# Attention output projection of an encoder layer: its first half in a fixed order by row blocks, with the last heads' values and turns between them

## The chip, the core and the metric

The kernel runs on one core of one Trainium2 chip. A core has four compute engines with instruction queues of their own: TensorE (matmuls and transposes; PE in the profile, its weight loads PEld), VectorE (DVE), ScalarE (ACT) and GpSimd (POOL). SyncE (SP) issues most of the transfers. Operands lie in the on-chip memory SBUF, matmul results in the eight banks of PSUM. The metric is the time of one execution on the device in microseconds (us); the median of several runs counts, lower is better.

## What is computed

One layer of a bidirectional encoder on 512 tokens of width 1024: two parallel mixers (a state-space branch and a gated MLP branch) merged by gates, then attention to 256 memory tokens, then a SwiGLU feed-forward part (FFN). The change lies in the attention:

```python
def memory_cross_attention(hn, memn, w_q, w_k, w_v, w_o):
    q = (hn @ w_q).reshape(bsz, seq, XATTN_HEADS, XATTN_HEAD_DIM)   # 512 x (4 heads x 256)
    k = (memn @ w_k).reshape(bsz, MEM_LEN, XATTN_HEADS, XATTN_HEAD_DIM)
    v = (memn @ w_v).reshape(bsz, MEM_LEN, XATTN_HEADS, XATTN_HEAD_DIM)
    s = jnp.einsum('blhd,bmhd->bhlm', q, k).astype(jnp.float32) * (XATTN_HEAD_DIM ** -0.5)
    p = jax.nn.softmax(s, axis=-1).astype(v.dtype)
    o = jnp.einsum('bhlm,bmhd->blhd', p, v).reshape(bsz, seq, D_MODEL)
    return o @ w_o
...
        h = h + memory_cross_attention(rms_norm(h, xattn_norm_g[i]), memn,
                                       w_q[i], w_k[i], w_v[i], w_xo[i])
        h = h + swiglu(rms_norm(h, ffn_norm_g[i]), w_gate[i], w_up[i], w_down[i])
    return rms_norm(h, final_norm_g)
```

## The kernel before

Every product is taken in three matmuls (`mm3`, L355): each operand is split into a high part, rounded to the type fp32r, and a low part, the rest; high times high, high times low and low times high are added up. `split` (L83) makes the parts: ACT casts the high one (L85), DVE subtracts it (L86). So each matrix that a product has made passes through ACT and DVE before the next product can read it.

The attention works by heads, four of them. `scores(hd)` (L1402) multiplies queries and keys, and ACT and DVE make the softmax in `prob`, token rows on the partitions. `turn_probs` (L1426) transposes `prob` on TensorE, four 128x128 transposes for each half of the memory tokens, eight for a head, into a bank `ppt`, and splits the result into `p_hi`, `p_lo`. `values` (L1436) multiplies the memory's values `vts` by them, for each of the two blocks of 128 columns of a head (`dt_`): six matmuls into a bank `po`, split into `ot_hi`, `ot_lo`. A head thus makes two of the eight blocks of k of the last product, `ot` times `w_xo`.

That product is done in two halves of 512 output columns. A half has four row blocks of 128 tokens (t), each summed in a bank of its own (`pt0` to `pt3`), and four weight blocks (wi) of two blocks of k each, one for a head. A row block with one weight block is six matmuls of 128x512 (`tok_block`, L431). The first half is done by `tokm` (L1512, L399), which takes the first two weight blocks for all rows, then the last two together for row after row. Between the weight blocks its `hooks` call `second` (values of head 1, turns of heads 2 and 3) and `last_two` (values of heads 2 and 3). At the end of a row `add_evac` (L1328) adds the bank to the residual `h` on DVE, and ACT sums its squares. The second half is written out below it (L1522 on), and goes two rows at a time; behind it come the norm, the transposes of its result (`ptr`) and the FFN.

Weights are taken from a list made beforehand. `next_w` (L330) hands out the next block and on the way issues loads, three blocks ahead, into a ring of three raw buffers (`wraw`), and splits, two blocks ahead, into a ring of three pairs `whi`, `wlo` (L107). A buffer comes free when the last instruction that reads it is done. Blocks 2 and 3 of the second half and the first FFN blocks lie in other buffers (`s`), in a pool that is opened where the heads' pool is closed (L1513 to L1515). SP's queue carries the loads and is in order, like each engine's; POOL's queue carries transfers that add onto a loaded tile, and one small operation of the norm (`r`).

PSUM has two rings: five banks `mm` (`bank`, L77), used by `psc`, `po`, `pt` and the products, and three banks `aux` (L80), used by the transposes.

The order on each engine's queue is not that of the code. A planner orders the instructions of each engine by a simulated clock: of those whose inputs it takes as ready, the one written first. `in_order` (`tc.keep_in_program_order`) pins an instruction behind the one that was written before it for the same engine. In the first half of w_xo nothing is pinned before the change. `tick` moves work of other stages forward; none is left here but a counter.

Of the kernel before, what the change touches and what calls it, by code (L numbers as in the profile page):

```python
# [17 lines left out]
P = 128  # L18
D = 1024
T = 512  # L20
NT = T // P
KD = D // P
M = 256
NM = M // P
# [28 lines left out]
def hybrid_layer_kernel(  # L53
# [8 lines left out]
    nc = tc.nc  # L62
    x, mem, out = x[0], mem[0], out[0]
    w_in, w_glu, w_proj_a, w_proj_b, w_out = w_in[0], s5_w_glu[0], w_proj_a[0], w_proj_b[0], w_out[0]
    w_q, w_k, w_v, w_xo = w_q[0], w_k[0], w_v[0], w_xo[0]
# [11 lines left out]
    def bank(name):  # L77
        return pm.tile([P, 512], F32, tag="mm", name=name)

    def aux(name, shape=(P, 512)):  # L80
        return pa.tile(list(shape), F32, tag="aux", name=name)
# [11 lines left out]
    in_order = tc.keep_in_program_order  # L93
# [261 lines left out]
    def mm3(ps, a, b, start, stop, free=False, turn=False):  # L355

        for i, (x, y) in enumerate(((0, 0), (0, 1), (1, 0))):
            m = nc.tensor.matmul(ps, a[x], b[y], start=start and i == 0, stop=stop and i == 2, skip_group_check=free)  # L358
            if turn:
                in_order(m)  # L360
# [38 lines left out]
    def tokm(w, c0, act, nk, evac, ntok=NT, last=2, kpt=2, hooks={}, cut=None, t0=0):  # L399


        toks = range(t0, t0 + ntok)
        ps = {t: bank(f"pt{t - t0}") for t in toks}
        nw = nk // kpt
        held = []
        full = slice(0, 512)
        for wi in range(nw):
            hi, lo = next_w(w, wi * kpt, kpt, c0, 512)
            held.append((wi, hi, lo))
            if wi in hooks:  # L410
                hooks[wi]()
            if wi < nw - last:
                todo, held = held, []
                for t in toks:
                    end = cut is not None and t == ntok - 1 and wi == nw - last - 1
                    tok_block(ps[t], t, todo, act, kpt, full, wi == 0, end)
                    if end:
                        cut(None, ps[t])
                tick(1.3 * ntok)
        for t in toks:  # L420
            if cut is not None and t == ntok - 1:
                for i in range(2):
                    p = aux("pcut", (P, 256))
                    tok_block(p, t, held, act, kpt, slice(256 * i, 256 * i + 256), True, True)
                    cut(i, p)
            else:
                tok_block(ps[t], t, held, act, kpt, full, nw == last, True)
                evac(t, ps[t])
            tick(1.3 * len(held))

    def tok_block(ps, t, ws, act, kpt, cs, first, final):  # L431
        tsl = slice(t * P, (t + 1) * P)
        for i, (wi, hi, lo) in enumerate(ws):
            for k in range(kpt):
                kk = wi * kpt + k
                mm3(ps, (act[0](kk, tsl), act[1](kk, tsl)) if callable(act[0]) else
                    (act[0][:, kk, tsl], act[1][:, kk, tsl]),
                    (hi[:, k, cs], lo[:, k, cs]), first and i == k == 0,
                    final and i == len(ws) - 1 and k == kpt - 1)

    side = {"gen": None, "credit": 0.0, "rate": 0.0, "now": 0, "later": []}

# [653 lines left out]
    for h in range(H):  # L1096
        ps = bank("psv")
# [230 lines left out]
    def add_evac(half, layer, fin, fin0=None):  # L1328

        def f(t, ps):  # L1330
            nc.vector.tensor_tensor(h[:, t, HALF[half]], h[:, t, HALF[half]], ps, ALU.add)
            sum_sq(hss[:, layer, t, half:half + 1], h[:, t, HALF[half]])
            if half == 1:
                fin(t, hss[:, layer, t, :])
            elif fin0 is not None:
                fin0(t)
        return f
# [85 lines left out]
                nc.vector.tensor_scalar(prob[:, 2 * i + tt, :], prob[:, 2 * i + tt, :], rs[:, tt:tt + 1], None, ALU.mult)  # L1423
        return prob

    def turn_probs(hd, prob):  # L1426
        p_hi = ap_.tile([P, NM, T], F32R, tag="p_hi", name="p_hi", bufs=2)
        p_lo = ap_.tile([P, NM, T], F32R, tag="p_lo", name="p_lo", bufs=2)
        for mt in range(NM):
            ps = aux("ppt", (P, NT, P))  # L1430
            for t in range(NT):
                nc.tensor.transpose(ps[:, t, :], prob[:, t, mt * P:(mt + 1) * P], ident)
            split(p_hi[:, mt, :], p_lo[:, mt, :], ps.rearrange("p t m -> p (t m)"))
        return p_hi, p_lo

    def values(hd, p_hi, p_lo):  # L1436
        for dt_ in range(2):
            ps = bank("po")
            cs = slice(hd * XD + dt_ * P, hd * XD + dt_ * P + P)
            for mt in range(NM):  # L1440
                mm3(ps, (vts[0][:, mt, cs], vts[1][:, mt, cs]), (p_hi[:, mt, :], p_lo[:, mt, :]), mt == 0, mt == NM - 1)
            split(ot_hi[:, 2 * hd + dt_, :], ot_lo[:, 2 * hd + dt_, :], ps)

    def query_product(ps, n, q, start=False):
# [5 lines left out]
    def turn(hd, probs):  # L1450
        pts[hd] = turn_probs(hd, probs)
# [43 lines left out]
    probs3 = scores(3)  # L1495
    turn(1, probs1)

    def second():
        values(1, *pts.pop(1))
        turn(2, probs2)  # L1500
        turn(3, probs3)

    def last_two():
        for i in (2, 3):
            values(i, *pts.pop(i))

    g_f = gain(ffn_norm_g[0], "g_f")
    ot = (ot_hi, ot_lo)
    fn_hi, fn_lo = token_slot("fn", AWAY)
    fn = (fn_hi, fn_lo)  # L1510

    tokm(w_xo, 0, ot, KD, add_evac(0, 1, None), hooks={1: second, 2: last_two})  # L1512
    at.close()  # L1513
    ff = ExitStack()
    fp = ff.enter_context(tc.tile_pool(name="ffn", bufs=1))  # L1515
# [330 lines left out]
```

## Time and profile before

| | us |
|---|---|
| median of 3 runs | 881.05 |
| fastest and slowest run | 880.0, 881.38 |
| the profiled execution | 883.48 |
| its span, first to last instruction | 881.7 |
| mean granted TensorE clock | 0.992 of full speed |

The span is that of the profiled execution alone, and its time is 1.8 us longer. All times of rows are microseconds from the span's start. A row of the timeline gives start, length, engine, line, operation, output and inputs, and in brackets the idle time of the engine just before it with what ended that. The length of a matmul's row is modelled and longer than its pace: rows of neighbouring matmuls overlap. A row of stretches gives start and end, length, and for each engine busy time and number of instructions, then the granted clock, the share of the DMA engines and GB/s.

### The profile page before, as it was taken

The numbers are of one execution on the slowest core, as the hardware profiler recorded it, in microseconds if no ns is written. First come the engines' busy times: TensorE is split into PE (matmuls) and PEld (weight loads), VectorE is DVE, ScalarE is ACT, GpSimd is POOL, SyncE is SP. The second block draws the span as 40 slices with busy tenths as digits, with TensorE's granted clock in tenths as the row PEclk, the third lists the DMA queues.
The fourth block names the chain that finished last, engine by engine and source line by source line (L and its number), as shares of the span: only waits on it lengthen the run. The fifth ranks groups of instructions, "written<-read, shape, count | busy, mean of one in ns | idle before, by whom it ended". The sixth has DMA issues, their size and how long they took to land.

```text
span 881.7 us, 14747 instructions
## 1 busy us (share of the span) xinstructions
PE 863.3 (98%) x5760; PEld 769.7 (87%) x5760; DVE 658.4 (75%) x1068; ACT 467.2 (53%) x692; POOL 86.4 (10%) x117
## 2 busy tenths in 40 slices
PE   8999999999998999999999999999999999999996
PEld 5788888888888988889899878999999999988875
DVE  5699885899845777658856836767878767899875
ACT  5643953244366553547555535645455455656664
POOL 1001301311000001100001001101211111000010
PEclk8999999999999999999999999999999999999999
DMA  7769565898664798735679645647999998366672
GB/s 239 197 191 298 104 179 148 183 234 193 166 195 115 241 285 258 245 112 156 207 218 256 172 108 159 168 123 168 228 232 236 211 239 215 96 187 207 193 237 96
DMA packets 117256, 169.56 MB, mean 192 GB/s; under 512 B 9265, under 2 KB 82497, under 8 KB 117058
## 3 DMA queue, kind: packets, MB, share of 16 engines
q1 hardware_dynamic: 97602, 141.64, 50.6%
q0 software_dynamic: 19296, 26.45, 19.2%
q8 instruction: 45, 0.74, 0.3%
q10 hardware_dynamic: 288, 0.52, 0.2%
q14 instruction: 25, 0.20, 0.1%
HBM read 159.71 MB, written 48.73 MB: 236 GB/s over the span
## 4 chain that ended last, share of the span: by engine, by line
PE 91%; DMA 4%; ACT 2%; DVE 2%; SPq 1%; issue 1%; POOL 0%; POOLq 0%; ACTq 0%; DVEq 0%
PE pf L358 26%; PE pt L358 17%; PE px L1146 12%; PE pq L1146 6%; PE dx L358 5%; PE dq L358 3%; PE pv L1146 3%; PE bx L1146 2%; PE qx L1146 2%; PE dv L358 2%; PE pz L889 2%; PE ptr L520 1%; PE po L358 1%; PE qv L1146 1%; DMA slab<-in_s_log_step_dram 1%; DMA wraw<-qsum 1%
## 5 line engine op out<-in xcount | busy, mean ns | idle before, releaser
L85 ACT CAST whi<-wraw 128x1024 fp32r<-128x1024 f32 (+1 forms) x145 | 148.6, 1025 | 158.0 <-PE pf L358 48.6
L86 DVE TENSOR_TENSOR wlo<-wraw,whi 128x1024 fp32r<-128x1024 f32 (+1 forms) x145 | 171.9, 1188 | 69.1 <-ACT whi L85 67.4
L358 PE MATMUL pf<-xn,whi 128*128 128x512 f32 x448 | 140.4, 393 | 0.0
L358 PEld LDWEIGHTS pf<-xn,whi 128*128 128x128 f32 x448 | 83.7, 188 | 17.5 <-issue 0.4
L358 PE MATMUL pf<-xn,wlo 128*128 128x512 f32 x224 | 87.8, 392 | 0.0
L1146 PE MATMUL px<-fn,whi 128*128 128x256 f32 x480 | 83.3, 276 | 0.0
L1146 PEld LDWEIGHTS px<-fn,whi 128*128 128x128 f32 x480 | 72.6, 188 | 0.2
L86 DVE TENSOR_TENSOR wlo<-b,whi 128x1024 fp32r<-128x1024 f32 x40 | 48.9, 1222 | 27.9 <-ACT whi L85 27.9
L85 ACT CAST whi<-b 128x1024 fp32r<-128x1024 f32 x40 | 42.2, 1054 | 50.8 <-PE px L1146 27.8
L1146 PE MATMUL px<-fn,wlo 128*128 128x256 f32 x240 | 66.4, 277 | 0.0
L1146 PE MATMUL pq<-s,whi 128*128 128x256 f32 x320 | 55.0, 276 | 0.0
L358 PE MATMUL dx<-whi,s 128*128 128x512 f32 x170 | 53.4, 391 | 0.4 <-DVE h L1771 0.4
L86 DVE TENSOR_TENSOR wlo<-t,whi 128x1024 fp32r<-128x1024 f32 x30 | 36.7, 1224 | 19.4 <-ACT whi L85 19.4
L85 ACT CAST whi<-t 128x1024 fp32r<-128x1024 f32 x30 | 31.6, 1053 | 35.3 <-PE pv L1146 12.4
L358 PEld LDWEIGHTS pf<-xn,wlo 128*128 128x128 f32 x224 | 42.1, 188 | 8.7 <-issue 0.2
L1146 PEld LDWEIGHTS pq<-s,whi 128*128 128x128 f32 x320 | 48.2, 188 | 0.0
L358 PE MATMUL pt<-whi,xn 128*128 128x512 f32 x128 | 44.6, 415 | 1.6 <-ACT xn L85 1.4
L1146 PEld LDWEIGHTS px<-fn,wlo 128*128 128x128 f32 x240 | 45.1, 188 | 0.0
L1146 PE MATMUL pq<-s,wlo 128*128 128x256 f32 x160 | 44.2, 276 | 0.0
L358 PEld LDWEIGHTS dx<-whi,s 128*128 128x128 f32 x170 | 31.8, 188 | 7.5 <-issue 0.8
L358 PE MATMUL dx<-wlo,s 128*128 128x512 f32 x85 | 33.1, 391 | 0.3 <-DVE wlo L86 0.3
L358 PEld LDWEIGHTS pt<-whi,xn 128*128 128x128 f32 x128 | 24.7, 195 | 7.8 <-ACT xn L85 2.0
(451 smaller groups left out, 2200.7 us busy)
## 6 DMA issues: line engine op xcount, KB each, us to landing
wraw<-in_w_in_dram SPq DMA_DIRECT2D x36, 512.0 KB, 4.6
dsum<-in_w_down_dram SPq DMA_DIRECT2D x20, 512.0 KB, 5.7
wraw<-dsum SPq DMA_DIRECT2D x20, 512.0 KB, 3.8
b<-in_w_gate_dram SPq DMA_DIRECT2D x15, 512.0 KB, 6.6
b<-in_w_up_dram SPq DMA_DIRECT2D x15, 512.0 KB, 5.6
wraw<-in_w_down_dram SPq DMA_DIRECT2D x15, 512.0 KB, 4.5
dsum<-in_w_down_dram POOLq DMA_DIRECT2D x10, 512.0 KB, 7.8
dsum<-dsum POOLq DMA_DIRECT2D x10, 512.0 KB, 7.6
```

The lines of the kernel that those rows point to most:

```text
L85: hi = nc.scalar.copy(dst_hi, src)
L86: lo = nc.vector.tensor_tensor(dst_lo, src, dst_hi.bitcast(F32), ALU.subtract)
L358: m = nc.tensor.matmul(ps, a[x], b[y], start=start and i == 0, stop=stop and i == 2, skip_group_check=free)
L520: nc.tensor.transpose(ps[:, j, :], src[:, k * P:(k + 1) * P], ident)
L889: nc.tensor.matmul(ps[:, g, :], wt[:, g, :], u[:, o * GO + g, :], start=True, stop=True)
L1146: nc.tensor.matmul(ps[:, j, :], a[x], b[y], start=start and j == k == i == 0, stop=k == 3 and i == 2, skip_group_check=True)
```

## The change

The first half of w_xo is no longer done by `tokm`. Its instructions on TensorE are written out and pinned, through a new argument `turn` of `tok_block`, `turn_probs` and `values`, which is handed on to `mm3` or to `in_order`. The order on TensorE becomes, with S(wi, t) a row block, V(hd, dt) a block of a head's values and T(hd) the eight transposes of a head:

```
S(0,0) V(1,0) S(0,1) V(1,1) S(0,2) T(2) S(0,3)
S(1,0) T(3) S(1,1) V(2,0) S(1,2) V(2,1) V(3,0) S(1,3) V(3,1)
S(2,0) S(3,0)  S(2,1) S(3,1)  S(2,2) S(3,2)  S(2,3) S(3,3)
```

The values written so take their bank from the ring `aux` of three and not from the ring of five. ACT, DVE, POOL and SP are not pinned, nor are the values of head 0, the turns of heads 0 and 1, the scores and the second half.

```diff
--- before.py
+++ after.py
@@ -428,7 +428,7 @@
                 evac(t, ps[t])
             tick(1.3 * len(held))
 
-    def tok_block(ps, t, ws, act, kpt, cs, first, final):
+    def tok_block(ps, t, ws, act, kpt, cs, first, final, turn=False):
         tsl = slice(t * P, (t + 1) * P)
         for i, (wi, hi, lo) in enumerate(ws):
             for k in range(kpt):
@@ -436,7 +436,7 @@
                 mm3(ps, (act[0](kk, tsl), act[1](kk, tsl)) if callable(act[0]) else
                     (act[0][:, kk, tsl], act[1][:, kk, tsl]),
                     (hi[:, k, cs], lo[:, k, cs]), first and i == k == 0,
-                    final and i == len(ws) - 1 and k == kpt - 1)
+                    final and i == len(ws) - 1 and k == kpt - 1, turn=turn)
 
     side = {"gen": None, "credit": 0.0, "rate": 0.0, "now": 0, "later": []}
 
@@ -1423,22 +1423,25 @@
                 nc.vector.tensor_scalar(prob[:, 2 * i + tt, :], prob[:, 2 * i + tt, :], rs[:, tt:tt + 1], None, ALU.mult)
         return prob
 
-    def turn_probs(hd, prob):
+    def turn_probs(hd, prob, turn=False):
         p_hi = ap_.tile([P, NM, T], F32R, tag="p_hi", name="p_hi", bufs=2)
         p_lo = ap_.tile([P, NM, T], F32R, tag="p_lo", name="p_lo", bufs=2)
         for mt in range(NM):
             ps = aux("ppt", (P, NT, P))
             for t in range(NT):
-                nc.tensor.transpose(ps[:, t, :], prob[:, t, mt * P:(mt + 1) * P], ident)
+                m = nc.tensor.transpose(ps[:, t, :], prob[:, t, mt * P:(mt + 1) * P], ident)
+                if turn:
+                    in_order(m)
             split(p_hi[:, mt, :], p_lo[:, mt, :], ps.rearrange("p t m -> p (t m)"))
         return p_hi, p_lo
 
-    def values(hd, p_hi, p_lo):
-        for dt_ in range(2):
-            ps = bank("po")
+    def values(hd, p_hi, p_lo, parts=(0, 1), turn=False):
+        for dt_ in parts:
+            ps = aux("po") if turn else bank("po")
             cs = slice(hd * XD + dt_ * P, hd * XD + dt_ * P + P)
             for mt in range(NM):
-                mm3(ps, (vts[0][:, mt, cs], vts[1][:, mt, cs]), (p_hi[:, mt, :], p_lo[:, mt, :]), mt == 0, mt == NM - 1)
+                mm3(ps, (vts[0][:, mt, cs], vts[1][:, mt, cs]), (p_hi[:, mt, :], p_lo[:, mt, :]), mt == 0, mt == NM - 1,
+                    turn=turn)
             split(ot_hi[:, 2 * hd + dt_, :], ot_lo[:, 2 * hd + dt_, :], ps)
 
     def query_product(ps, n, q, start=False):
@@ -1495,21 +1498,40 @@
     probs3 = scores(3)
     turn(1, probs1)
 
-    def second():
-        values(1, *pts.pop(1))
-        turn(2, probs2)
-        turn(3, probs3)
-
-    def last_two():
-        for i in (2, 3):
-            values(i, *pts.pop(i))
-
     g_f = gain(ffn_norm_g[0], "g_f")
     ot = (ot_hi, ot_lo)
     fn_hi, fn_lo = token_slot("fn", AWAY)
     fn = (fn_hi, fn_lo)
 
-    tokm(w_xo, 0, ot, KD, add_evac(0, 1, None), hooks={1: second, 2: last_two})
+    fin = add_evac(0, 1, None)
+    ps = {t: bank(f"pt{t}") for t in range(NT)}
+    held = []
+
+    def out_rows(wi, t):
+        tok_block(ps[t], t, held[wi:wi + 1], ot, 2, slice(0, 512), wi == 0, wi == 3, True)
+
+    def head_values(hd, dt_):
+        values(hd, *pts[hd], parts=(dt_,), turn=True)
+
+    def head_turn(hd, prob):
+        pts[hd] = turn_probs(hd, prob, True)
+
+    between = {(0, 0): lambda: head_values(1, 0), (0, 1): lambda: head_values(1, 1),
+               (0, 2): lambda: head_turn(2, probs2), (1, 0): lambda: head_turn(3, probs3),
+               (1, 1): lambda: head_values(2, 0),
+               (1, 2): lambda: (head_values(2, 1), head_values(3, 0)), (1, 3): lambda: head_values(3, 1)}
+    for wi in range(2):
+        held.append((wi,) + next_w(w_xo, 2 * wi, 2, 0, 512))
+        for t in range(NT):
+            out_rows(wi, t)
+            tick(1.3)
+            between.get((wi, t), lambda: None)()
+    held += [(wi,) + next_w(w_xo, 2 * wi, 2, 0, 512) for wi in (2, 3)]
+    for t in range(NT):
+        out_rows(2, t)
+        out_rows(3, t)
+        fin(t, ps[t])
+        tick(2.6)
     at.close()
     ff = ExitStack()
     fp = ff.enter_context(tc.tile_pool(name="ffn", bufs=1))
```

## The prediction

> **What bounds the kernel now.** I read the page's first part and its chain of waits first, then a table of stretches around the changed stage, and last the instructions of that stage in order of time. The page says that TensorE works nearly all the span and that the chain runs along it.
>
> ```profile
> PE 863.3 (98%) x5760; PEld 769.7 (87%) x5760; DVE 658.4 (75%) x1068; ACT 467.2 (53%) x692; POOL 86.4 (10%) x117
> PE 91%; DMA 4%; ACT 2%; DVE 2%; SPq 1%; issue 1%; POOL 0%; POOLq 0%; ACTq 0%; DVEq 0%
> ```
>
> The table of stretches (start:end, length, then busy time and count by engine) places the stage: the first half of w_xo runs from 495.5 to 529.7, the second half to 553.4, then the FFN.
>
> ```profile
> core 0: us, PE busy (x) PEld busy (x) DVE busy (x) ACT busy (x) POOL busy (x), PEclk, DMA share, GB/s
> 495.50:529.70 34.20, 33.26 (x154) 26.33 (x153) 16.39 (x30) 14.17 (x28) 2.35 (x2) 1.00 0.48 121
> 529.70:553.40 23.70, 23.70 (x114) 19.65 (x113) 15.72 (x27) 12.86 (x26) 2.98 (x4) 1.00 0.58 159
> 553.40:600.00 46.60, 46.60 (x408) 46.55 (x407) 34.78 (x38) 25.31 (x35) 4.34 (x4) 1.00 0.54 147
> 600.00:700.00 100.00, 100.00 (x885) 100.00 (x884) 77.25 (x78) 52.07 (x63) 14.00 (x13) 1.00 0.91 217
> ```
>
> Behind 529.7 TensorE is never idle here, so a stage that ends x us sooner or later moves the end by x, and nothing that only reaches the other engines sooner is worth anything. Within the stage TensorE is idle for 0.94 us by these rows; that and the pace of its matmuls is all that this change can win.
>
> In order of time (start, length, engine, line, operation; an idle time in brackets) the stage holds these places:
>
> ```profile
> 495.53 0.39 PE L358 MATMUL pt<-whi,ot_hi 128*128 128x512 f32 x1
> 496.90 0.60 PE L1432 MATMUL ppt<-ident,prob 128*128 128x128 f32 x4
> 501.87 0.48 PE L358 MATMUL po<-p_hi,vt 128*128 128x512 f32 x1
> 503.78 0.60 PE L1432 MATMUL ppt<-ident,prob 128*128 128x128 f32 x4
> 504.65 0.50 PE L358 MATMUL pt<-whi,ot_hi 128*128 128x512 f32 x1 [0.27 <-ACT ot_hi L85]
> 513.27 0.39 PE L358 MATMUL po<-p_hi,vt 128*128 128x512 f32 x1
> 514.34 0.50 PE L358 MATMUL pt<-whi,ot_hi 128*128 128x512 f32 x1 [0.68 <-ACT ot_hi L85]
> 525.80 0.39 PE L358 MATMUL po<-p_hi,vt 128*128 128x512 f32 x1
> 528.83 1.07 PE L358 MATMUL pt<-whi,ot_lo 128*128 128x512 f32 x4
> 529.74 0.39 PE L358 MATMUL pt<-whi,ot_hi 128*128 128x512 f32 x1
> 529.74:543.34 13.60, 13.60 (x61) 11.21 (x60) 8.37 (x15) 5.66 (x14) 1.89 (x2) 1.00 0.86 237
> 514.34:529.74 15.40, 15.40 (x67) 12.27 (x68) 6.14 (x8) 5.20 (x7) 1.14 (x1) 1.00 0.63 167
> ```
>
> The first row is the stage's first matmul, the last instruction row the first of the second half: 34.21 us. The last two rows are stretches with no transposes; a count holds one instruction that belongs to the neighbour, so they give 13.60/60 = 0.2267 us for a matmul that runs row block by row block, and 15.40/66 = 0.2333 where the stage goes block of k by block of k, changing bank every other matmul. Both waits are for ot_hi: a head's values had been computed in the one bank left of five, and w_xo ran into them.
>
> **The change, part by part.** No arithmetic is added or removed: 96 matmuls into pt, 36 into po and 20 transposes of head 1 (second half), 2 and 3, before and after. What changes is who stands behind whom on TensorE.
>
> *The two waits.* The bracketed 0.27 and 0.68 are less than the loss, since a matmul's row is longer than its pace. Four transposes take 4 x 0.11 = 0.44 us (the price below), so L358 could have gone on at 504.22 and went at 504.65: 0.43. After the row at 513.27 it could have gone at 513.50 and went at 514.34: 0.84. In the new order the values of a head stand at least one other block ahead of their use, so I take out 0.43 + 0.84 = 1.27. To check the cover, a split of one such result:
>
> ```profile
> 508.62 0.59 ACT L85 CAST ot_hi<-po 128x512 fp32r<-128x512 f32 x1 [4.02 <-PE po L358]
> 509.24 0.69 DVE L86 TENSOR_TENSOR ot_lo<-po,ot_hi 128x512 fp32r<-128x512 f32 x1 [3.20 <-ACT ot_hi L85]
> ```
>
> The high part is there 0.65 us after the last matmul, the low part after 1.35. Head 1's second value block has two blocks and eight transposes between it and its use (6 x 0.2267 x 2 + 0.88 = 3.6 us), head 2's has three blocks (4.1), head 3's last one has nine matmuls (2.0 us) before its k comes. All are covered; without that cover each would cost 1.35.
>
> *The banks.* Values go from the ring of five (four are held by pt) to the ring of three of the transposes. Their order there is: two of head 1's transposes, two of its values, two and two transposes, four values. Each takes a bank that was filled three allocations earlier, and the nearest reuse (head 3's second transposes behind head 2's first) lies 2 x 1.36 + 0.88 = 3.6 us after it, against the 1.35 of a split. I cost it at nothing.
>
> *The new wait.* Each pinned instruction stands behind the one written before it, and the first stands behind head 1's last transpose. So the four transposes now at 496.90 go first, at 495.53, and one row block later TensorE meets head 1's values, which today come at 501.87 behind four row blocks. They need p_hi and p_lo of head 1:
>
> ```profile
> 493.68 0.61 DVE L1423 TENSOR_SCALAR prob<-prob,rs 128x256 f32<-128x256 f32 x2
> 497.65 1.07 ACT L85 CAST p_hi<-ppt 128x512 fp32r<-128x512 f32 x2
> 498.22 0.62 DVE L1423 TENSOR_SCALAR prob<-prob,rs 128x256 f32<-128x256 f32 x2
> 498.75 1.28 DVE L86 TENSOR_TENSOR p_lo<-ppt,p_hi 128x512 fp32r<-128x512 f32 x2
> 490.00:498.75 8.75, 8.75 (x68) 8.15 (x66) 8.68 (x28) 6.27 (x23) 1.22 (x1) 1.00 0.61 158
> ```
>
> Head 1's probabilities are ready at 494.3, so the transposes do not wait. But ACT casts p_hi at 497.65 behind the exponentials of heads 2 and 3, and VectorE has the whole softmax of heads 2 and 3 ahead of p_lo: first half out at 498.75 + 0.68 = 499.43. The order of ACT and DVE is not pinned; softmax is written before the turn and keeps its place, so I keep these times. TensorE: transposes to 495.97, first row block to 497.33, first value matmul at 498.2 behind p_hi, second at 499.47 behind p_lo. Unhindered that second would go at 497.56: **a wait of 1.91 us**. Behind it on TensorE stand three row blocks that need nothing from head 1; behind those, ACT's casts of ot and the release of w_xo's buffers. From below: if p_hi and p_lo went ahead of heads 2 and 3 on ACT and DVE, the chain is 495.98 + 0.59 + 0.68 = 497.3 and the wait is nothing. I take 1.91, as these rows are of the same instructions.
>
> *Pace.* Row block by row block is the order of the second half, 0.2267; the upper bound is 0.2333. Transposes from here:
>
> ```profile
> 543.34 1.04 PE L520 MATMUL ptr<-ident,xs 128*128 128x128 f32 x8
> 544.45 0.39 PE L358 MATMUL pt<-wlo,ot_hi 128*128 128x512 f32 x1
> ```
>
> Eight and one matmul take 1.11 us, so 0.11 each. The stage becomes 132 x 0.2267 + 20 x 0.11 + 1.91 = 29.92 + 2.20 + 1.91 = 34.03, against 34.21: **0.18 us less**. At 0.2333 it would be 34.9, 0.7 more.
>
> *Weights and queues.* w_xo's four blocks and the second half's first two share three buffers, each freed by the last row block that uses it.
>
> ```profile
> 501.94 1.05 ACT L85 CAST whi<-wraw 128x1024 fp32r<-128x1024 f32 x1 [3.22 <-PE pt L358]
> 522.97 1.05 ACT L85 CAST whi<-wraw 128x1024 fp32r<-128x1024 f32 x1 [0.34 <-PE pt L358]
> 524.05 1.23 DVE L86 TENSOR_TENSOR wlo<-wraw,whi 128x1024 fp32r<-128x1024 f32 x1 [0.70 <-ACT whi L85]
> 525.30 0.37 SPq L137 DMA_DIRECT2D wraw<-in_w_gate_dram  x1
> 534.34 1.34 POOL L181 DMA_DIRECT2D t<-in_w_gate_dram x1 [13.09 <-DMA t<-in_w_gate_dram]
> ```
>
> The first (block 3 of w_xo) moves to about 507, with 13 us to spare. The second is the second half's block 1: it waits for block 2's last use, now one row block (1.36) before the stage's end, and is split 1.05 + 1.23 later, 1.0 us into the second half, where its first use is 12 matmuls (2.7 us) in. Cost nothing; with one more split ahead (2.3) it would be 0.6. On SP the load of w_gate at 525.30 waits for that split and comes some 5 us later, and POOL's accumulation at 534.34 waits for a load behind it; their uses lie behind 553, so 20 us hide it. The pool of the heads, in whose place units' tiles lie, is freed eight row blocks before the stage's end, at about 529.6 - 10.9 = 518.7, in place of 526.2 (behind the po row at 525.80), so some loads come sooner.
>
> **The rivals.** *A, the forecast*: 881.05 - 0.18 = 880.9. The profiled run took 883.48 with a span of 881.7; I move the median of the runs by the same difference. With a wait of 1.2 to 1.9 and either pace A spans 880.1 to 881.8.
>
> *B, the wait doesn't come*: the order on ACT and DVE lets head 1 through, and the pace is the quick one: 34.03 - 1.91 = 32.12, 2.1 us less, 879.0. For it speaks that the transposes now run 1.4 us sooner; against it that VectorE is busy in all 8.75 us up to 498.75 but 0.07 (the last row of that fence).
>
> *C, the wait brings the clock down*, the slower side. After another wait the granted clock fell:
>
> ```profile
> 279.56 0.38 PE L1146 MATMUL qv<-yb_hi,whi 128*128 128x256 f32 x1 [1.85 <-ACT qv L1159]
> 277.24:280.65 3.41, 1.55 (x14) 1.36 (x13) 3.00 (x5) 3.22 (x5) 0.00 (x0) 1.00 0.37 75
> 280.65:284.06 3.41, 3.41 (x18) 3.41 (x18) 2.06 (x3) 1.62 (x3) 0.00 (x0) 0.50 0.70 195
> 263.58:266.99 3.41, 1.95 (x29) 1.70 (x29) 0.69 (x1) 0.00 (x0) 0.00 (x0) 1.00 0.92 278
> ```
>
> With 1.86 of 3.41 us idle, the next 3.41 us ran at 0.50, worth 1.7 us; with 1.46 idle it stayed at 1.00. The new wait has one matmul inside it: by busy time (0.39 for that matmul, and the 0.16 by which a row outlasts its pace) it is idle for 1.6, between the two. If it decides so, A + 1.7 = 882.6, up to 883.3 with the slow pace.
> The Trainium skill (TensorE: Matmul & The Clock Gate, "Part 1: The HAM clock gate (the "warmup" mystery)") says the clock falls after at least one idle window of about 3.4 us, and that windows run free of the kernel. The trace agrees on the length (3.41 at 0.50) and not on the trigger (1.86 idle was enough); by the page's trigger C would have no chance and the time would be A's.
>
> *D, the second half's norm is crowded*: splits of FFN weights, ready sooner, get ahead of the rows' add, square and scale on ACT and DVE.
>
> ```profile
> 540.16 1.42 DVE L512 SCALAR_TENSOR_TENSOR xs<-h,r,g_f 128x512 f32<-128x512 f32 x2 [0.73 <-POOL r L497]
> ```
>
> Row 0 is scaled at 541.6 and transposed at 543.34 (above): 1.76 to spare. A split is 1.05 + 1.23 = 2.28, so 0.5 lost for each of four rows, 2.0 in all: 882.9. It decides only where one falls ahead of every row; today the same splits fall between them unharmed.
>
> **How the numbers follow.** What this kernel's measurement can tell from no change is about 0.2%, 1.76 us: 879.29 to 882.81. A 0.43, B 0.15, C 0.25, D 0.12, and 0.05 for an order of the rest that I have not seen. Faster: nearly all of B and a little of A, 0.15. Slower: half of C (its price straddles the bound), most of D and the rest, 0.28. The remaining 0.57 is within. The range reaches from B to C's upper end: 879.0 to 883.3.
>
> **What would show it.** Right: four transposes ahead of the first pt; a wait of about 1.9 at the first po for p_hi and p_lo of head 1; no wait for ot_hi; 0.227 a matmul; the second half starting 34.0 us after the first pt. Wrong: p_lo of head 1 ahead of heads 2 and 3 on DVE (B); granted clock under 1.00 in the 4 us behind the wait (C); idle time before ptr, or before 553 at all (D). A wait for a bank at po, or for w_xo's block 1 of the second half, would make the sum itself wrong.

## The result, and the profile after

| | us |
|---|---|
| changed kernel, median of 22 runs | 883.88 (879.99 to 887.32) |
| kernel before, median of 22 runs beside it | 879.67 (877.88 to 883.25) |
| ratio | 1.0041, 95% interval 1.0030 to 1.0053 |
| profiled execution of the changed kernel, its span | 884.59, 882.8 |

The change makes the kernel slower, by 0.41%, about 3.6 us (the two medians alone lie 4.2 apart). The forecast was no change, 880.9 with a range that ended at 883.3.

The page's first part and its chain of waits, of the changed kernel:

```profile
PE 862.7 (98%) x5760; PEld 768.6 (87%) x5760; DVE 659.0 (75%) x1068; ACT 467.2 (53%) x692; POOL 86.4 (10%) x117
PE 88%; DMA 5%; DVE 3%; ACT 2%; issue 1%; SPq 1%; POOL 0%; POOLq 0%; ACTq 0%
```

TensorE does the same work in the same busy time (863.3 before). But its share of the chain falls from 91% to 88%, and VectorE's and the transfers' grow: TensorE waits more, and a total of busy time cannot show where.

The table of stretches does. Three stretches stand here for the kernel before and then for the changed one: the first half of w_xo, most of the second half, and the rest up to the first `pf` matmul of the FFN that reads `whi`, here called the mark. The first half is taken by count, 152 matmuls from the first on, and 273 more lead to the mark, in every kernel of this document. The cut between the second and the third stretch is not at the same matmul in the two kernels (before, it is the end of the second half; after, two matmuls ahead of it), so only these two together can be compared. The sum row gives the length of all three.

```profile
495.53:529.74 34.21, 33.27 (x155) 26.31 (x154) 16.41 (x29) 14.18 (x28) 2.35 (x2) 1.00 0.48 121
529.74:553.38 23.64, 23.64 (x113) 19.64 (x112) 15.66 (x27) 12.80 (x26) 2.98 (x4) 1.00 0.58 159
553.38:572.15 18.77, 18.77 (x162) 18.72 (x161) 14.12 (x18) 11.87 (x19) 1.87 (x2) 1.00 0.66 169
sum 76.62, PE 75.68 PEld 64.66 DVE 46.19 ACT 38.85 POOL 7.20; mean PE 25.23 PEld 21.55 DVE 15.40 ACT 12.95 POOL 2.40
```

```profile
494.14:527.68 33.54, 32.98 (x154) 26.71 (x153) 16.48 (x30) 14.02 (x30) 2.51 (x2) 1.00 0.49 140
527.68:551.31 23.63, 23.18 (x108) 18.62 (x106) 14.49 (x23) 10.20 (x20) 2.25 (x3) 1.00 0.51 121
551.31:573.61 22.30, 20.64 (x171) 19.52 (x169) 14.02 (x20) 14.45 (x24) 2.43 (x3) 1.00 0.57 157
sum 79.47, PE 76.80 PEld 64.85 DVE 44.99 ACT 38.67 POOL 7.19; mean PE 25.60 PEld 21.62 DVE 15.00 ACT 12.89 POOL 2.40
```

The first half is what the change is about, and it is 0.67 us shorter (34.21 to 33.54). All of the loss lies behind it: from there to the mark it is 45.93 us against 42.41, 3.52 more. Over the three stretches that makes 2.85 us; what follows them is as long as before (309.2 and 309.6 us, span less the mark). The sum of these stretches is called "the stage" below, and it is the better measure of single executions, since the time ahead of it differs by up to 6 us between profiles.

In order of time, the changed kernel's first half. Head 1's turns go first, and its values wait for `p_lo`:

```profile
494.14 0.60 PE L1432 MATMUL ppt<-ident,prob 128*128 128x128 f32 x4
495.19 1.10 ACT L85 CAST p_hi<-ppt 128x512 fp32r<-128x512 f32 x2
495.96 0.39 PE L358 MATMUL po<-p_hi,vt 128*128 128x512 f32 x1
496.75 0.50 PE L358 MATMUL po<-p_lo,vt 128*128 128x512 f32 x1 [0.40 <-DVE p_lo L86]
497.08 0.62 PE L358 MATMUL po<-p_hi,vt 128*128 128x512 f32 x2
497.14 0.68 DVE L86 TENSOR_TENSOR p_lo<-ppt,p_hi 128x512 fp32r<-128x512 f32 x1
497.87 0.50 PE L358 MATMUL po<-p_lo,vt 128*128 128x512 f32 x1 [0.16 <-DVE p_lo L86]
```

By pace the first low part is 496.75 - 496.19 = 0.56 late, the second 497.87 - 497.53 = 0.34: 0.9 us, and no other wait follows in this half. The step behind such a wait is longer as well, 0.33 (496.75 to 497.08) in place of 0.2267. Then the second half, where block 1's parts come late:

```profile
519.77 0.49 SPq L137 DMA_DIRECT2D wraw<-in_w_gate_dram  x1
518.00:530.00 12.00, 12.00 (x55) 9.91 (x54) 4.91 (x6) 2.89 (x6) 2.49 (x2) 1.00 1.05 301
530.86 1.05 ACT L85 CAST s<-wraw 128x1024 fp32r<-128x1024 f32 x1 [3.01 <-DMA wraw<-in_w_gate_dram]
531.81 0.63 ACT L486 ACTIVATE sq<-h 128x512 f32<-128x512 f32 x1
532.43 1.03 ACT L85 CAST whi<-wraw 128x1024 fp32r<-128x1024 f32 x1
532.89 0.39 PE L358 MATMUL pt<-whi,ot_lo 128*128 128x512 f32 x1
533.52 1.21 PE L358 MATMUL pt<-whi,ot_hi 128*128 128x512 f32 x4 [0.24 <-ACT whi L85]
534.95 0.50 PE L358 MATMUL pt<-wlo,ot_hi 128*128 128x512 f32 x1 [0.21 <-DVE wlo L86]
```

The buffer that block 1 needs is free at 527.84, when the last matmul that reads block 2 ends (it starts at 527.45). The cast starts 4.6 us later, behind a cast of w_gate's part that itself waited 3.01 us for its load, and behind a square. That load was issued at 519.77, 25.6 us into the stage; before the change it was 29.8 (525.30). It took 11 us to land, where before it took 4 (its cast went at 529.25). Five other loads had been issued in the 2.8 us ahead of it, three of them for the units that lie in the heads' pool's place, which now comes free sooner, and the transfers were busy throughout: a share of 1.05 from 518 to 530, against 0.66 before. That the crowd made the load slow is likely; no run shows it.

By pace the two waits cost 0.40 + 0.52 = 0.92. That they cost no more is the planner's work. Timeline rows leave out buffer numbers, but the program's own order has them: row 0's block 0 went at 518.84 to 520.43, in the middle of the first half, so that the first half's last six matmuls stand right behind its count (527.68 to 529.04), and from 529.04 to 533.12 it is block 0 of rows 1, 2 and 3. Rows 2 and 3 were laid ahead of block 1, and that is missed at the other end, at the norm:

```profile
551.62 0.40 PE L358 MATMUL pt<-s,ot_lo 128*128 128x512 f32 x1
551.77 1.23 DVE L86 TENSOR_TENSOR s<-wraw,s 128x1024 fp32r<-128x1024 f32 x1 [0.34 <-ACT s L85]
552.28 0.66 PE L520 MATMUL ptr<-ident,xs 128*128 128x128 f32 x4 [0.26 <-ACT full L524]
553.25 0.50 PE L358 MATMUL pf<-fn,s 128*128 128x256 f32 x2 [0.32 <-ACT fn L85]
553.51 1.41 DVE L512 SCALAR_TENSOR_TENSOR xs<-h,r,g_f 128x512 f32<-128x512 f32 x2
553.59 0.28 PE L1146 MATMUL px<-fn,whi 128*128 128x256 f32 x1
554.41 0.63 PE L520 MATMUL ptr<-ident,xs 128*128 128x128 f32 x4 [0.54 <-DVE xs L512]
554.84 1.28 DVE L86 TENSOR_TENSOR fn<-ptr,fn 128x512 fp32r<-128x512 f32 x2
555.58 2.78 PE L358 MATMUL pf<-fn,s 128*128 128x256 f32 x22 [0.55 <-DVE fn L86]
```

Four waits. With 0.2267 us for a 512 wide matmul and 0.11 for a transpose or a 256 wide one they cost 0.43, 0.53, 0.71 and 0.73: 2.40 us. Two of them have a common reason on VectorE: row 2's scaling (`xs`, 553.51) stands ahead of row 1's low parts (`fn`, 554.84), for which the FFN's 22 matmuls wait; and row 2's transposes, laid ahead of these matmuls, wait for that `xs`. In the kernel before, VectorE had them the other way round, and TensorE did not wait:

```profile
552.60 0.69 DVE L86 TENSOR_TENSOR fn<-ptr,fn 128x512 fp32r<-128x512 f32 x1
553.20 1.41 DVE L512 SCALAR_TENSOR_TENSOR xs<-h,r,g_f 128x512 f32<-128x512 f32 x2
554.53 1.22 DVE L86 TENSOR_TENSOR s<-wraw,s 128x1024 fp32r<-128x1024 f32 x1
```

The last row is a split of FFN weights; it stood behind row 1's `fn` and row 2's `xs`, and in the changed kernel (551.77) it stands ahead of both. Its cast on ACT (550.71) likewise stands ahead of the copies `full` (551.65) and the casts of `fn` (552.60), for which the first two of the four waits are. No run moves this split alone, so its share of the four waits stays open.

So the account is -0.67 + 0.92 + 2.40 = 2.65 of the 2.85 us; the rest is small steps, such as those behind the waits.

### The profile page after: what moved, and what is told of

It is laid out like the page before. It is cut to its first block, busy times and chain, and to the rows that moved or that the text cites. A ratio compares the mean times of both kernels' runs of the same rounds, so it can differ in the third digit from the quotient of the medians.

```text
span 882.8 us, 14747 instructions
## 1 busy us (share of the span) xinstructions
PE 862.7 (98%) x5760; PEld 768.6 (87%) x5760; DVE 659.0 (75%) x1068; ACT 467.2 (53%) x692; POOL 86.4 (10%) x117
## 4 chain that ended last, share of the span: by engine, by line
PE 88%; DMA 5%; DVE 3%; ACT 2%; issue 1%; SPq 1%; POOL 0%; POOLq 0%; ACTq 0%
PE pf L358 24%; PE pt L358 14%; PE px L1146 12%; PE dx L358 7%; PE pq L1146 6%; PE dq L358 3%; PE pv L1146 3%; PE qx L1146 2%; PE bx L1146 2%; PE dv L358 2%; PE qv L1146 1%; PE pz L889 1%; DMA slab<-in_s_log_step_dram 1%; DMA wraw<-in_w_gate_dram 1%; PE qq L1146 1%; PE po L358 1%
```

## The experiments

The traces tell where TensorE waits, not what each wait hangs on. Theories in the expectations: 1, rows 2 and 3 laid ahead take the norm's cover, and the late cast is the smaller part, both of them from block 2's buffer, which comes free late; 2, all is the late cast; 3, it is the ring of three banks. 4 to 6 came with later results and are told there. The numbers in the labels have gaps (3 and 9 are not used). Stage is in us by the profiled execution, and the ratio is to the kernel before on the same chip.

| run | first half | behind it | stage | less before | ratio, 95% interval |
|---|---|---|---|---|---|
| kernel before | 34.21 | 42.41 | 76.62 | | |
| changed kernel | 33.54 | 45.93 | 79.47 | +2.85 | 1.0041 (1.0030 to 1.0053) |
| e1 cast first | 33.43 | 46.43 | 79.86 | +3.24 | 1.0033 (1.0011 to 1.0055) |
| e2 block by block | 33.55 | 42.26 | 75.81 | -0.81 | 0.9998 (0.9976 to 1.0019) |
| e4 ring only | 32.49 | 47.83 | 80.32 | +3.70 | 1.0034 (1.0014 to 1.0054) |
| e5 order only | 35.63 | 43.36 | 78.99 | +2.37 | 1.0036 (1.0016 to 1.0056) |
| e6 rows not ahead | 33.38 | 48.35 | 81.73 | +5.11 | 1.0055 (1.0032 to 1.0077) |
| e7 cast first, rows not ahead | 33.35 | 43.98 | 77.33 | +0.71 | 1.0000 (0.9980 to 1.0020) |
| e8 block by block, values later | 32.96 | 42.15 | 75.11 | -1.51 | 0.9976 (0.9959 to 0.9993) |
| e10 rows ahead alone | 33.24 | 43.43 | 76.67 | +0.05 | 0.9999 (0.9979 to 1.0019) |
| e11 norm order | 33.72 | 44.72 | 78.44 | +1.82 | 1.0011 (0.9992 to 1.0031) |
| e12 cast first, norm order | 33.52 | 43.86 | 77.38 | +0.76 | 1.0003 (0.9983 to 1.0023) |

Stage and ratio agree: times 880, each ratio less 1 is within 0.9 us of the stage's difference. A stage is of one execution, and the same instructions differ by some tenths between executions (the first half of e2 and of e10, with the same order on TensorE, by 0.31).

**e1: the cast alone.** On the changed kernel the cast of w_gate's part may not stand ahead of block 1's on ACT (`issue_after` keeps what is written in it behind the named instruction).

```diff
+            if behind is not None:
+                with tc.issue_after(casts[behind].ins):
+                    return halves(got.pop("raw"), place)
...
-            plan_block(w_gate, 4 * i, 4, FS, 256, place=i + 1)
+            plan_block(w_gate, 4 * i, 4, FS, 256, place=i + 1, behind=(1, None)[i])
```

> The changed kernel, but the gate weights' cast into s may not stand ahead of the cast of the second half's weight block 1 on ACT; TensorE's order is that of the changed kernel. Theory 1 (TensorE runs the first weight block of rows 2 and 3 ahead of block 1, so the norm at the end has 12 matmuls less to hide behind; the late cast is only a smaller part): the waits for whi and wlo go, 0.9 us of the loss, about 2.5 us stay: +2.7 us against before. Theory 2 (all of it is the late cast): -0.7 us against before. Theory 3 (the ring of three banks): +3.6, as the changed kernel.

The waits for `whi` and `wlo` are gone, the planner still lays rows 2 and 3 ahead, and the norm's waits stay as they were. Theory 2 falls. In this execution they also brought the clock down: the same 22 matmuls as in the last row above now take 4.38 us in place of 2.78.

```profile
557.84 4.38 PE L366 MATMUL pf<-fn,s 128*128 128x256 f32 x22 [0.54 <-DVE fn L87]
```

**e2: the buffer.** The changed kernel, with the last two weight blocks of the first half taken one after the other over all rows, in place of both for each row. Block 2 is then last read four row blocks ahead of the half's end, not one.

```diff
-    for t in range(NT):
-        out_rows(2, t)
-        out_rows(3, t)
-        fin(t, ps[t])
-        tick(2.6)
+    for wi in (2, 3):
+        for t in range(NT):
+            out_rows(wi, t)
+            if wi == 3:
+                fin(t, ps[t])
+            tick(1.3)
```

> The changed kernel, but the last two weight blocks go one after the other over all four rows, so that block 2's buffer comes free 4 row blocks (5.4 us) before the half ends and not one. TensorE's order in the second half is then that of the kernel before. Theory 1: no wait for block 1, no matmul of rows 2 and 3 ahead, the loss is gone and the 0.7 us won in the first half stay: -0.7 us against before. Theory 2: the same, as the cast is early too. Theory 3 (the ring): +3.6.

Block 1 of the second half is cast at 520.37, 5.2 us ahead of the half's end at 525.61:

```profile
520.37 1.05 ACT L85 CAST whi<-wraw 128x1024 fp32r<-128x1024 f32 x1 [3.94 <-PE pt L358]
```

Rows 2 and 3 are not laid ahead, and no wait is left behind the first half, which is as long as in the changed kernel (33.55). This one edit takes 3.66 us off the changed kernel's stage and 0.4% off its ratio. That points to the moment at which block 2's buffer comes free as the root of the loss. The edit also moves the ends of the first half's rows, and with them their adds and squares; no run separates the two.

**e4 and e5: the two parts of the change alone.** e4 is the kernel before with the values of heads 1 to 3 in the ring of three and nothing pinned; e5 is the changed kernel with its values in the ring of five.

```diff
-            ps = bank("po")
+            ps = aux("po") if hd else bank("po")
```

```diff
-            ps = aux("po") if turn else bank("po")
+            ps = bank("po")
```

> The kernel before, with one part of the change alone: values of heads 1 to 3 in the ring of the transposes' banks, nothing pinned. In its order TensorE again takes rows 2 and 3 ahead in the second half, and the gate's cast stands ahead of block 1's. Theory 1: about +2.5 to +3.5 us against before, with idle time before the transposes of the norm. Theory 3 (the ring itself costs): a wait for a bank at the values, about +3.6. If the fixed order is what costs: 0.

> The changed kernel, with the other part alone: the fixed order, values in the ring of five banks as before. Eleven of the twelve matmuls of rows 2 and 3 are still taken ahead, but block 1's cast stands ahead of the gate's. Theory 1: the waits for block 1 go, the loss of the norm's cover stays in part, +1.5 to +2.7 us against before, plus some tenths where two values stand next to each other on one bank (0.6 to 1.4 us). Theory 2: -0.7 plus that wait, 0 to +0.7. Theory 3: the same as theory 2.

By the ratios each part alone costs about as much as both, but not at the same place. In e4, with the fifth bank no longer holding it up, the planner by itself lays the row blocks so that block 2 is read almost to the end, and the same waits follow: 0.51 and 0.25 for block 1, the four of the norm, the half clock behind them. The first half of e4 is the shortest of all, 1.72 us under the kernel before, and what is behind it 5.42 longer. No values wait for a bank in e4, so theory 3 falls. In e5 block 1's cast stands ahead of w_gate's and its waits are gone; behind the first half it is 0.95 longer than before, with two waits at the norm (0.48 and 0.34). The other 1.42 lies in the first half, where two blocks of values follow each other in one bank, and the second waits:

```profile
515.87 0.50 PE L358 MATMUL po<-p_hi,vt 128*128 128x512 f32 x1 [1.40 <-DVE ot_lo L86]
```

That is the wait that the ring of three takes away.

**e6 and e7: rows 2 and 3 not ahead.** On the changed kernel (e6) and on e1 (e7) the first weight block of rows 2 and 3 may not go ahead of block 1 of row 1.

```diff
-                tok_block(ps[t], t, held[wi:wi + 1], ot, 2, slice(0, 512), wi == 0, False)
+                with tc.issue_after(row1.ins) if t0 == 2 and wi == 0 else ExitStack():
+                    tok_block(ps[t], t, held[wi:wi + 1], ot, 2, slice(0, 512), wi == 0, False)
...
```

> The changed kernel, with the first weight block of rows 2 and 3 of the second half not allowed ahead of row 1's last matmul that is laid there in the program, block 1 of row 1. The cast of w_gate's part is still ahead of block 1's cast on ACT. Theory 1 (two costs that trade against each other): TensorE now stands at block 1 and waits for its high part (there at about 532.5, needed at 530.4 by the changed kernel's times) and its low part (534.9), some 3 to 4 us idle; the four waits of the norm (0.26, 0.32, 0.54, 0.55) are gone. Together 2.5 to 4 us over the kernel before. Theory 4 (the late cast costs only what the brackets of the changed kernel show, 0.45, and the rest is the order of rows 2 and 3): the kernel before or 0.5 under it.

> Both edits on the changed kernel: the cast of w_gate's part not ahead of block 1's cast on ACT, and rows 2 and 3 not ahead of row 1. Block 1's buffer is freed by the first half's next to last row block, 1.36 us before the stage's end, and its split takes 1.05 + 1.23, so its low part comes about 1 us into the second half, 1.7 us before its first use. Theory 1: no wait for block 1, none at the norm, only that at head 1's values: 0.7 us under the kernel before. If the norm's waits do not hang on that order they stay, and it is 2.5 to 3.5 over.

In both the norm's waits are gone, so they hang on these rows. In e6 TensorE stands at block 1 instead, for longer than theory 1 had (5.1 us over before, not 2.5 to 4), since that wait also brings the clock down. The two rows of e6, then a window of its table of stretches right behind them, at a granted clock of 0.50:

```profile
531.72 0.73 PE L359 MATMUL pt<-whi,ot_hi 128*128 128x512 f32 x2 [3.19 <-ACT whi L85]
533.15 0.50 PE L359 MATMUL pt<-wlo,ot_hi 128*128 128x512 f32 x1 [0.70 <-DVE wlo L86]
```

```profile
533.65:537.06 3.41, 3.41 (x10) 2.63 (x9) 1.23 (x1) 0.07 (x1) 0.00 (x0) 0.50 0.85 277
```

So the planner's choice in the changed kernel was the better of two bad ones, by the stage (2.85 against 5.11); the intervals of the two ratios overlap. Theory 4, by which the late cast costs only its 0.45, falls. For e7 no wait was expected, and two remained:

```profile
528.16 0.63 ACT L496 ACTIVATE sq<-h 128x512 f32<-128x512 f32 x1 [1.33 <-DVE h L1341]
528.79 1.03 ACT L85 CAST whi<-wraw 128x1024 fp32r<-128x1024 f32 x1
529.87 0.73 PE L367 MATMUL pt<-whi,ot_hi 128*128 128x512 f32 x2 [0.62 <-ACT whi L85]
531.13 0.50 PE L367 MATMUL pt<-wlo,ot_hi 128*128 128x512 f32 x1 [0.53 <-DVE wlo L87]
```

Block 2 is last read by a matmul from 526.15 to 526.54, one row block ahead of the first half's last one (527.51); the cast starts at 528.79, since ACT has squares of the first half's rows ahead of it, and these wait for the row's add. With the buffer freed so late there is no room even for that.

**e10: rows 2 and 3 ahead, alone.** The kernel of e2, where all casts are in time, with block 0 of the second half written for all four rows ahead of block 1.

```diff
-        ps = {t: bank(f"pt{t - t0}") for t in (t0, t0 + 1)}
-        for wi in range(2):
...
+        if t0 == 0:
+            held.append((0,) + next_w(w_xo, 0, 2, 512, 512))
+            for t in range(NT):
+                ps4[t] = bank(f"pt{t % 2}")
+                tok_block(ps4[t], t, held[:1], ot, 2, slice(0, 512), True, False)
+            held.append((1,) + next_w(w_xo, 2, 2, 512, 512))
...
```

> The second experiment's kernel (the first half weight block by weight block, the casts in time), with the second half's first weight block written for all four rows ahead of block 1: what the planner did in the changed kernel, here with no late cast. It prices that order alone. Theory 1: no wait for block 1's whi or wlo, but the norm of rows 2 and 3 has 2.7 us less of matmuls to lie behind: waits ahead of ptr and pf of 0.25 to 0.55, four of them, 2 to 3 us of TensorE's time, and the half clock behind them in part of the executions; 2 to 3.5 us over the kernel before. Theory 2 (all is the late cast): 0.7 under the kernel before, no such waits.

Here theory 1 was wrong in its size. The norm does wait, at two places in place of four, and the stage is 0.86 us longer than e2's, not 2 to 3 (behind the first half alone, 1.17):

```profile
549.39 0.50 PE L358 MATMUL pf<-fn,s 128*128 128x256 f32 x2 [0.45 <-ACT fn L85]
550.39 2.78 PE L358 MATMUL pf<-fn,s 128*128 128x256 f32 x22 [0.39 <-DVE fn L86]
```

In e10 row 1's low parts stand ahead of row 2's scaling on VectorE (549.66 and 550.86), as in the kernel before. That gave theory 5: the other half of the norm's loss is this order. Theory 6: the norm is late whatever the order.

**e11 and e12: the order on VectorE.** On the changed kernel (e11) and on e1 (e12) row 2's scaling may not stand ahead of row 1's last low part of `fn`.

```diff
-        rms_scale(src, g, xs, ss)
+        with tc.issue_after(row1[0].ins) if hold[0] and tsl.start == 2 * P else ExitStack():
+            rms_scale(src, g, xs, ss)
...
```

> The changed kernel, with row 2's scaling (xs, two instructions on VectorE) not allowed ahead of row 1's last low parts of fn; in the changed kernel they stood ahead (553.51 against 554.84), and row 2's first transposes stood ahead of the FFN's first 22 matmuls on TensorE and now stand behind them. The tenth experiment priced rows 2 and 3 ahead alone at 0.86 us over the second experiment, where the changed kernel is 3.7 over it, about 0.9 of it by the waits for block 1. Theory 5 (the rest, about 1.9, is this order on VectorE: the norm is crowded, and row 2's work stands ahead of row 1's): the waits of 0.54 for xs and 0.55 for fn shrink to one of under 0.45, 1.4 to 2 us off the changed kernel, 1 to 2 us over the kernel before. Theory 6 (the norm's chain itself is late, its order makes no difference): the same waits in another place, 3 to 3.7 over the kernel before.

> The same edit on the first experiment's kernel, whose cast of block 1 is in time for the rows laid ahead: no wait for block 1, and row 2's scaling behind row 1's low parts. Theory 5: no half clock behind the norm, waits at pf of 0.3 to 0.45 alone; within 0.9 us of the kernel before, on either side. Theory 6: as the first experiment, 3 to 3.7 over.

The wait for `xs` is gone and the one for `fn` is 0.39, in both kernels. The timeline of e11 at the norm:

```profile
552.98 1.28 DVE L88 TENSOR_TENSOR fn<-ptr,fn 128x512 fp32r<-128x512 f32 x2
553.72 2.86 PE L361 MATMUL pf<-fn,s 128*128 128x256 f32 x22 [0.39 <-DVE fn L88]
555.24 2.74 DVE L515 SCALAR_TENSOR_TENSOR xs<-h,r,g_f 128x512 f32<-128x512 f32 x4 [0.66 <-POOL r L500]
```

The stage is 1.03 us shorter than the changed kernel's; e12's is 2.48 shorter than e1's, of which 1.60 is the half clock (4.38 - 2.78) and 0.88 the order. Behind the first half alone the order is worth 2.57 - 1.60 = 0.97 by e12, and 1.21 by e11, where block 1's waits are some 0.2 shorter too. Theory 5 holds at about 1 us, less than the 1.4 to 2 expected. Theory 6 falls. e11's ratio alone cannot be told from no change.

**e8: both mended.** The kernel of e2, with head 1's values and head 2's turn one row block later, so that head 1's `p_lo` has 1.36 us more.

```diff
-    between = {(0, 0): lambda: head_values(1, 0), (0, 1): lambda: head_values(1, 1),
-               (0, 2): lambda: head_turn(2, probs2), (1, 0): lambda: head_turn(3, probs3),
+    between = {(0, 1): lambda: head_values(1, 0), (0, 2): lambda: head_values(1, 1),
+               (0, 3): lambda: head_turn(2, probs2), (1, 0): lambda: head_turn(3, probs3),
```

> The first half weight block by weight block (block 2's buffer free four row blocks sooner, as in the second experiment) and head 1's two value blocks and head 2's turn one row block later. p_hi and p_lo of head 1 then have 1.36 us more, so the wait of 0.40 + 0.16 at its first values is gone, about 0.9 us of pace. Theory 1: no wait over 0.2 us from the first w_xo matmul to the FFN's w_up; 1.0 to 1.7 us under the kernel before. If the wait only moves (p_lo later still, or a wait for the low part of head 1's second block ahead of weight block 1), 0 to 0.7 under.

The values no longer wait; one wait of 0.31, at head 3's last transposes for a bank that head 2's `p_lo` still reads, takes the place of 0.56 in brackets, and the first half is 32.96 us, 0.6 shorter than e2's. It is the one kernel whose interval lies below 1: 0.24% faster than the kernel before (0.07 to 0.41), 2.1 us.

## Why the prediction was wrong

- **The two waits for `ot_hi`**: right. None is left, and no value block waits for a bank of the ring of three (also right).
- **The new wait**: right in place and cause, mis-sized: 1.91 forecast, 0.9 measured. I had kept the order of ACT and VectorE; in fact ACT cast `p_hi` ahead of its last exponentials and VectorE took `p_lo` between the softmax's scalings. Rival B's mechanism came half true.
- **Pace**: nearly right. 0.2267 x 132 + 2.20 + 0.9 = 33.0, measured 33.54; 0.2 of the rest is the longer step behind the two waits, the other 0.3 small steps. For the first half the forecast was 0.18 us less, and it was 0.67.
- **Weights and queues: the step that failed.** "Cost nothing; with one more split ahead (2.3) it would be 0.6" was said of block 1 of the second half. The release was right: one row block ahead of the first half's end at 529.04. What is behind it was not. The cast waits not for the buffer alone but for its turn on ACT, behind a cast that waits for a load and behind squares that wait for adds; its low part was used 5.9 us into the half (534.95 - 529.04), where the forecast had the split in at 1.0. The forecast for that load was wrong too: it had it some 5 us later, behind block 1's split, and safe; it was issued 4 us sooner, counted from the stage's start, took 11 us and stood in block 1's way. That some loads come sooner was written down, and costed as harmless. By the brackets this looks like a slip of 0.45 us. It was not, since the planner answers a late input by another order: it laid rows 2 and 3 ahead, and that took the matmuls from in front of the norm.
- **What the lateness cost**: behind the first half the changed kernel is 3.67 us longer than e2, and the runs between them split this into four steps: rows 2 and 3 ahead, 1.17 (e10 less e2); row 1's transposes waiting for ACT's copies `full`, 0.25 in brackets, which e12 has and e10 has not, 0.43 (e12 less e10); VectorE's order, 0.97 (e1 without its half clock, less e12); block 1 itself, 1.10 (the changed kernel less e1 without its half clock; 0.92 by pace). They add up because each run is subtracted from the next; each is of one execution, and the cause of the second is argued from its wait alone.
- **Why the kernel before did not have it**: it has the same loop in the code, rows with both blocks. But nothing was pinned, the planner laid k by k over all four rows, and block 2 was last read some 7 us ahead of the half's end at 529.74 (its successor was cast at 522.97, in the prediction's rows). The pins made the order that the code had always said come true. I read the code for the release in the new order, and costed it, but not what the order before had given.
- **Rival C** had the right mechanism at the wrong wait: the half clock did not come behind head 1's values (granted 1.00 there in all profiles of the changed kernel's order) but behind the norm's waits, in e1 and e4, where it costs 1.6 us, and not in the changed kernel's own profile. A trigger between 1.46 and 1.86 us idle in a window, on which C rested, is not borne out (last section). That it comes in a part of the changed kernel's executions, and so makes up the 3.6 us of the ratio over the 2.85 of the stage, is possible and not shown.
- **Rival D** had the right place, the second half's norm, the right sign and a like size (2.0 against 2.40). Its cause, FFN weights' splits ahead of the rows, is there in part: one such split stands ahead of row 1's `fn` and row 2's `xs`, and did not before (551.77 and 554.53 above). e10, e11 and e12 have it ahead too and no run moves it; what e11 and e12 price is row 2's own work ahead of row 1's. That the size came close is luck as far as shown. D stood at 0.12, and with it I gave the chance of slower as 0.28, too little.

## What to carry to other kernels

When an order is pinned, list for every ring buffer the last reader before and after, and follow the next user of that buffer through its engine's queue to its first use; "free in time" is not "cast in time". Under a planner a late input need not show as one long wait: look for what was laid in the gap, and ask which later wait has lost that work as its cover. Small bracketed waits at one place (0.45 here) can thus stand for more than 2 us at another.

## What the runs showed of the hardware

TensorE's granted clock can fall after a stretch that is idle only in part, and whether it does depends on where the idle time lies, not on its amount alone. The changed kernel and e1 have the same four waits, and TensorE's busy time falls short by like amounts over them. Of e1, the window of 3.41 us ahead of the fall and the next:

```profile
554.76:558.17 3.41, 2.01 (x13) 1.36 (x12) 3.41 (x6) 2.75 (x7) 0.00 (x0) 1.00 0.46 132
558.17:561.58 3.41, 3.41 (x18) 3.41 (x17) 2.36 (x6) 1.41 (x3) 0.55 (x1) 0.50 1.10 364
```

Of the changed kernel, two windows around its norm, laid 79 and 80 lengths of 3.413 behind the half clock's start at 280.92, then that one and the one ahead of it:

```profile
550.57:553.98 3.41, 2.72 (x16) 1.72 (x14) 3.04 (x7) 3.40 (x8) 0.55 (x1) 1.00 0.49 151
553.98:557.40 3.42, 2.45 (x19) 2.24 (x20) 2.87 (x7) 2.68 (x6) 0.41 (x1) 1.00 0.97 313
280.92:284.33 3.41, 3.41 (x18) 3.41 (x18) 2.80 (x4) 2.28 (x4) 0.00 (x0) 0.50 0.76 206
277.51:280.92 3.41, 1.54 (x14) 1.35 (x13) 3.00 (x4) 3.40 (x5) 0.00 (x0) 1.00 0.13 27
```

In e1 three of the four fall into one window, 1.40 us idle, and the next runs at 0.50. In the changed kernel the window's edge at 553.98 cuts them into 0.69 and 0.97 idle, and the clock stays. The Trainium skill (TensorE: Matmul & The Clock Gate, "Part 1: The HAM clock gate (the "warmup" mystery)") says that such windows of 3413 ns run free of the kernel, and these rows agree, as far as 80 lengths within one execution can show it; it also says that the clock falls after a whole idle window, and here 1.40 of 3.41 was enough.

The idle share does not decide by itself either: in the prediction's rows a window with 1.46 idle kept the clock, one with 1.86 lost it, and here one with 1.40 loses it. Nor does the busy time of weight loads, the second pair of columns. Of e10, the window 176 lengths ahead of its half clock's start at 874.77, and the next:

```profile
274.03:277.44 3.41, 1.54 (x15) 1.35 (x13) 2.96 (x4) 3.38 (x6) 0.00 (x0) 1.00 0.06 13
277.44:280.85 3.41, 3.41 (x30) 3.41 (x31) 2.58 (x4) 2.18 (x4) 0.00 (x0) 1.00 0.79 219
```

With 1.54 and 1.35 busy, as in the changed kernel's window at 277.51, the clock stays here and fell there. What is counted stays open.
